# Rows of the delta rule's 16x16 blocks spread over their partitions by TensorE products in place of a round trip through DRAM

## Chip, cores and metric

One core of a Trainium2 chip. The metric is the device time in microseconds of one execution. TensorE is called PE here, VectorE DVE, ScalarE ACT, GpSimd POOL; SP only issues DMAs.

## What is computed

A trunk of two layers on 512 tokens of width 1024. The change lies in the first layer's mixer, in the chunked gated delta rule of its four heads. Cut to what matters here:

```
kk    = einsum('bhncd,bhnsd->bhncs', k * beta, k) * decay
a_mat = where(strictly lower, kk, 0) + eye
rhs   = concatenate([v * beta, k * beta * exp(gc)])
sol   = triangular_solve(a_mat, rhs, lower, unit_diagonal)
u, w  = sol[..., :dv], sol[..., dv:]
```

The rest of the layer (differential attention, output projection, MLP) and the second layer are the same code in both kernels.

## The kernel before

Weights come from HBM as float32, and ACT and DVE split each into a high and a low part in the fast matmul format (`whl`); a product is three matmuls of 512 or 256 columns. The trunk runs nearly all of its time on PE.

The first layer's mixer is `even_mixer` (lines 322 to 789). It is a list of generators that a planner at its end (lines 754 to 788) runs one step at a time while the program is built. `fill` holds the projections (q, k and v of the delta-rule heads: `project_a`, `values_a`; of the attention heads: `project_b`, `diff_values`; the output gates: `project_z`). `chains` holds the steps of each head. A chain's step says with `yield n` that its next step is due n * 1.55 us (`LAT_A`) of planned PE time later; `PE.time` (lines 82 to 94) adds up the matmuls' planned durations, four cycles a column for float32. Whenever no chain is due the planner takes a step of the next projection. So a `yield` decides how much projection work stands between two steps of a head. The order in which an engine then runs its instructions is near to this order, not equal to it: the building of the program moves an instruction ahead where its inputs and a buffer are there.

Four delta-rule heads work in pairs, 0 with 1 and 2 with 3. In `gdn_head`, line 502 finishes `lc`: for each of the 128 rows of a head's four token tiles, the 16 values of its row in the diagonal 16x16 block (128 partitions x 2 heads x 4 tiles x 16 columns). The second head of a pair then starts `small_inverses` for both (line 505). This inverts the 16x16 unit triangles by back substitution, and for it every partition needs all 16 rows of its block, not only its own: the tile `lb`, 128 partitions x 16 rows x 128 values. Before, `lb` is made by one DMA that writes `lc` to a DRAM tile `lsc` and eight DMAs that read it back, each broadcast to 16 partitions, all nine issued from ACT's queue (lines 435 to 441), followed by `yield 10.0`. Then 30 POOL instructions (lines 445 to 448), each needing the one before, turn `xc` into the inverses, with `lb` and `xc` as inputs; then `yield 10.0`, and the pair counts as solved. Its heads spread `xc` into block-diagonal tiles `x` on POOL (line 535, four instructions a head), PE transposes them (line 542), and three levels of products (line 551 on) join the blocks.

Things that share an engine or a buffer with this: the attention heads' rotation, of which one multiplication is on POOL (`rot`, line 706) between ACT's copies (line 702) and DVE's addition (line 707); the masks `ub` on POOL (lines 558, 563); `rs_t` on POOL (line 257); the tag `st` with five buffers (`N_ST`); the PSUM tag `ax` with two banks (`aux()`), which nearly every step of a delta-rule head uses.

Of the kernel before, what the change touches and what calls it, by code (L numbers as in the profile page):

```python
# [10 lines left out]
F32 = mybir.dt.float32  # L11
F32R = mybir.dt.float32r
I32 = mybir.dt.int32
AF = mybir.ActivationFunctionType
ALU = mybir.AluOpType
# [3 lines left out]
P = 128  # L19
# [17 lines left out]
BASE = 16  # L37
# [60 lines left out]
def trunk(ctx: ExitStack, tc: tile.TileContext, I, cst, out):  # L98
    nc = tc.nc
    V, S, G, PE = nc.vector, nc.scalar, nc.gpsimd, Tensor(tc)  # L100
# [10 lines left out]
    def acc():  # L111
        return pmm.tile([P, T], F32, tag="mm", name="mm")

    def aux():
        return pax.tile([P, T], F32, tag="ax", name="ax", bufs=2)
# [20 lines left out]
    def small(w, name):  # L136
        return smp.tile([P, w], F32, tag=f"sm{w}", name=name)
# [184 lines left out]
    def even_mixer(act, first, wba):  # L322
        w_in = I["w_in_even"][0]
        with ExitStack() as es:
# [4 lines left out]
            def st_(name):  # L329
                return gp.tile([P, T], F32, tag="st", name=name, bufs=N_ST)  # L330
# [1 line left out]
            def dtmp(name):  # L332
                return gp.tile([P, T], F32, tag="d", name=name, bufs=3)

            dp = es.enter_context(tc.tile_pool(name="dp", bufs=1, space=bass.MemoryType.DRAM))

            gmask = gp.tile([P, (N_MASK - 4) * P], F32, name="gmask")
            nc.scalar.dma_start(gmask, cst[:, 3 * P:(N_MASK - 1) * P])
            gm = {n: gmask[:, j * P:(j + 1) * P] for j, n in enumerate(CONST_NAMES[3:-1])}
# [8 lines left out]
            st, eye = {}, ccol[:, C_EYE:C_EYE + BASE]  # L348
# [84 lines left out]
            def small_inverses(pair):  # L433

                lc, n = small_l[pair], 2 * NT
                lsc = dp.tile([P // BASE, BASE * n * BASE], F32, tag="lsc", name="lsc", bufs=1)
                nc.scalar.dma_start(lsc.rearrange("b (r n) -> b r n", r=BASE), lc.rearrange("p h i c -> p (h i c)"))
                lb = gp.tile([P, BASE, n, BASE], F32, tag="lb", name="lb", bufs=1)
                for a in range(P // BASE):
                    nc.scalar.dma_start(lb[a * BASE:(a + 1) * BASE].rearrange("p r i c -> p (r i c)"),  # L440
                                        lsc[a:a + 1, :].broadcast_to([BASE, BASE * n * BASE]))
                yield 10.0
                xc = small_w[pair].rearrange("p h i c -> p (h i) c")
                tmp = gp.tile([P, n, BASE], F32, tag="xt", name="xt", bufs=1)
                for c in range(BASE - 1, 0, -1):
                    G.tensor_tensor(out=tmp[:, :, 0:c], in0=lb[:, c, :, 0:c],
                                      in1=xc[:, :, c].broadcast_to([P, n, c]), op=ALU.mult)
                    G.tensor_tensor(out=xc[:, :, 0:c], in0=xc[:, :, 0:c], in1=tmp[:, :, 0:c], op=ALU.add)
                yield 10.0
                solved.append(pair)  # L450

            def gdn_head(h, qT, kT):
# [51 lines left out]
                if second:  # L504
                    spawn(small_inverses(pair), 0.5)
# [268 lines left out]
            while chains or fill:  # L774
                due = [c for c in chains if c[0] <= PE.time]
                free = [f for f in fill if f[0]()]
                if due:
                    c = min(due, key=lambda c: c[0])
# [615 lines left out]
    with tc.tile_pool(name="ip", bufs=1) as ip:  # L1394
# [18 lines left out]
        ps = acc()  # L1413
# [3 lines left out]
        for i in range(NT):  # L1417
# [3 lines left out]
            r, ok, ss = small(1, "rx"), small(1, "ok"), ssx[:, i:i + 1]  # L1421
# [6 lines left out]
            if i == 2:  # L1428
                ps = acc()
# [10 lines left out]
        for k in range(KT):  # L1440
# [5 lines left out]
            w = cols[:, R_MIX + k:R_MIX + k + 1]  # L1446
# [9 lines left out]
    for layer in range(2):  # L1456
        if layer == 0:
            heads = even_mixer(act, first, wba)
            w, pairs = I["w_out_even"][0], (0, 2, 3, 1)
            xp = pools["x"] = ctx.enter_context(tc.tile_pool(name="xp", bufs=1))  # L1460
            for i in range(NT):
                x_tok.append(xp.tile([P, D], F32, name=f"x_tok{i}"))
                nc.sync.dma_start(x_tok[i], I["x"][0, i * P:(i + 1) * P, :])
        else:
            heads = odd_mixer(xs, last_tile)
            w, pairs = I["w_out_odd"][0], range(4)
        with tc.tile_pool(name=f"np{layer}", bufs=1) as pool:
            norm = Norm(pool, I["norm_mlp"][layer:layer + 1, :], 2)
            act, last_tile = out_proj(w, heads, norm, pairs)
        xs, halves, pj, last_tiles = mlp(layer, act, last_tile)  # L1470
        with tc.tile_pool(name=f"qp{layer}", bufs=1) as pool:
            if layer == 0:
                norm = Norm(pool, I["norm_mix"][1:2, :], 2)
            else:
                norm = Norm(pool, I["norm_final"].unsqueeze(0), 3)
            last_tile = ple(layer, xs, halves, pj, last_tiles, pool, norm)
# [24 lines left out]
```

## Time and profile before

| | us |
|---|---|
| median of 3 runs (1419.45 to 1420.86) | 1419.63 |
| the profiled execution, its own time | 1421.96 |
| span of the profiled execution, first to last instruction | 1420.2 |
| PE busy in it | 1384.1 (97%) |
| DVE busy | 867.3 (61%) |
| ACT busy | 773.5 (54%) |
| POOL busy | 174.2 (12%) |

Times in rows are microseconds from the start of the span. Matmuls overlap, and their ends are modelled, so that durations of neighbours can add up to more than their stretch: idle time of PE is read from the bracket of a row, and the price of a matmul from the distance between two starts. A bracket at the end of a row is the idle time of the engine before it and what ended it. In a stretch, "x" is the count of instructions that begin in it, and PEclk the share of full speed that the clock granted (1.00 is 2.4 GHz, 0.50 is 1.2 GHz). "PEld" is PE's weight load, "ACTq" an issue of a DMA by ACT's queue.

### The profile page before, as it was taken

To read this page: it belongs to the slowest core of one execution; us is meant where nothing else is said; L and a number is where in the kernel's file an instruction comes from. 1 tells how busy PE (TensorE), PEld (TensorE's weight loads), DVE (VectorE), ACT (ScalarE), POOL (GpSimd) and SP (SyncE) were. 2 spreads that over 40 slices of the span, in tenths; PEclk is the share of its full clock that TensorE was granted. 3 is DMA by queue.
4 is the path that set the end of the run, shared out by engine and by line. 5 is a ranking of instruction groups with operands and counts; after the bars stand their busy time and mean duration, and the time that the engine had idled before them with its cause. 6 is when DMAs were issued, how large, how long until landed. Compare 5 with 4: busy or idle time off the path is not lost. (4 is left out here: it accounts for less than half of the span.)

```text
span 1420.2 us, 18495 instructions
## 1 busy us (share of the span) xinstructions
PE 1384.1 (97%) x6969; PEld 1152.2 (81%) x6969; DVE 867.3 (61%) x1535; ACT 773.5 (54%) x1304; POOL 174.2 (12%) x231
## 2 busy tenths in 40 slices
PE   8999987999999999999999999999999999999997
PEld 6887775777888888888878888888888888888887
DVE  6837786665465665657665746646646565655865
ACT  6746775663555564556534545535355555554643
POOL 1350056010110201101001000000011020101100
PEclk9999998999999999999999999999999999999999
DMA  6251213114954856566333443852295476756611
GB/s 179 79 106 46 60 31 77 45 55 168 250 135 136 176 154 160 140 159 129 93 72 60 60 89 60 79 97 90 89 270 135 132 153 174 159 143 146 132 60 60
DMA packets 134238, 164.61 MB, mean 116 GB/s; under 512 B 9650, under 2 KB 91396, under 8 KB 133892
## 3 DMA queue, kind: packets, MB, share of 16 engines
q1 hardware_dynamic: 113968, 123.82, 32.6%
q0 software_dynamic: 15360, 33.56, 13.8%
q10 hardware_dynamic: 4820, 6.05, 1.9%
q8 instruction: 55, 0.90, 0.3%
q14 instruction: 35, 0.29, 0.1%
HBM read 152.78 MB, written 2.23 MB: 109 GB/s over the span
## 5 line engine op out<-in xcount | busy, mean ns | idle before, releaser
L90 PE MATMUL mm<-act,whl 128*128 128x512 f32 (+1 forms) x2784 | 657.9, 389 | 2.6 <-DVE whl L149 1.9
L90 PEld LDWEIGHTS mm<-act,whl 128*128 128x128 f32 x2784 | 506.3, 190 | 103.0 <-DVE whl L149 3.2
L90 PE MATMUL ax<-swhl,sa 128*128 128x512 f32 x1344 | 314.0, 389 | 0.0
L90 PEld LDWEIGHTS ax<-swhl,sa 128*128 128x128 f32 x1344 | 252.1, 188 | 52.4
L149 DVE TENSOR_TENSOR whl<-raw,whl 128x1024 fp32r<-128x1024 f32 x139 | 170.6, 1228 | 167.5 <-ACT whl L146 164.7
L149 DVE TENSOR_TENSOR swhl<-sraw,swhl 128x1024 fp32r<-128x1024 f32 x112 | 136.9, 1222 | 124.4 <-ACT swhl L146 124.2
L146 ACT ACTIVATE whl<-raw 128x1024 fp32r<-128x1024 f32 (+1 forms) x140 | 147.9, 1057 | 54.5 <-PE mm L90 50.2
L146 ACT ACTIVATE swhl<-sraw 128x1024 fp32r<-128x1024 f32 x112 | 118.8, 1060 | 101.2 <-PE ax L90 86.7
L90 PE MATMUL mm<-whl,act 128*128 128x256 f32 (+2 forms) x720 | 108.0, 307 | 0.2 <-ACT act L146 0.2
L1261 ACT ACTIVATE r<-mm 128x512 f32<-128x512 f32 x64 | 38.2, 597 | 126.0 <-PE mm L90 125.9
L90 PEld LDWEIGHTS mm<-whl,act 128*128 128x128 f32 x720 | 97.0, 190 | 6.7 <-ACT act L146 0.7
L1165 POOL DMA_DIRECT2D sraw<-w_mlp_down x48 | 57.5, 1218 | 251.0 <-DVE swhl L149 115.6
L319 DVE TENSOR_TENSOR x_tok<-x_tok,ax 128x512 f32<-128x512 f32 x114 | 73.5, 681 | 10.8 <-PE ax L90 10.7
L90 PE MATMUL mm<-owhl,act 128*128 128x256 f32 (+1 forms) x336 | 57.9, 329 | 0.0
L90 PE MATMUL mm<-owhl,hl 128*128 128x512 f32 x228 | 54.8, 397 | 0.0
L90 PEld LDWEIGHTS mm<-owhl,act 128*128 128x128 f32 x336 | 49.6, 188 | 6.4
L312 POOL TENSOR_TENSOR rn<-tn,nhalf 128x1 f32<-128x1 f32 x12 | 6.6, 553 | 385.9 <-DVE tn L311 385.9
L1165 POOL DMA_DIRECT2D sraw<-sraw x16 | 14.6, 915 | 302.5 <-DVE swhl L149 276.2
L90 PEld LDWEIGHTS mm<-owhl,hl 128*128 128x128 f32 x228 | 42.4, 188 | 10.1
L1174 ACT ACTIVATE sraw<-sraw 128x1024 f32<-128x1024 f32 x32 | 33.8, 1058 | 27.0 <-DVE swhl L149 17.5
L146 ACT ACTIVATE act<-ax 128x512 fp32r<-128x512 f32 x40 | 22.4, 595 | 43.1 <-PE ax L94 42.9
L149 DVE TENSOR_TENSOR sa<-hl,sa 128x512 fp32r<-128x512 f32 x64 | 43.8, 685 | 0.0
(341 smaller groups left out, 1609.6 us busy)
## 6 DMA issues: line engine op xcount, KB each, us to landing
raw<-w_mlp_up SPq DMA_DIRECT2D x64, 512.0 KB, 4.3
sraw<-w_mlp_down SPq DMA_DIRECT2D x64, 512.0 KB, 3.9
sraw<-w_mlp_down POOLq DMA_DIRECT2D x48, 512.0 KB, 5.8
raw<-w_in_even SPq DMA_DIRECT2D x32, 256.0 KB, 3.5
sraw<-sraw POOLq DMA_DIRECT2D x16, 512.0 KB, 6.3
raw<-w_ple_gate SPq DMA_DIRECT2D x16, 512.0 KB, 4.9
raw<-w_in_odd SPq DMA_DIRECT2D x16, 512.0 KB, 5.2
raw<-w_in_odd SPq DMA_DIRECT2D x32, 256.0 KB, 6.6
```

What stands on the lines that cost most here:

```text
L90: return self.tc.nc.tensor.matmul(out, lhsT=lhsT, rhs=rhs, start=start, stop=stop, skip_group_check=onto)
L146: S.activation(out=hi, in_=src, func=AF.Copy)
L149: return (E or V).tensor_tensor(out=lo, in0=src, in1=hi.bitcast(F32), op=ALU.subtract)
L312: G.tensor_tensor(out=r, in0=t, in1=nhalf[:, 0:1], op=ALU.pow)
L319: V.tensor_tensor(out=x_tok[i][:, cs], in0=x_tok[i][:, cs], in1=ps, op=op)
L1165: G.dma_start(o, t, accum_op=ALU.add)
L1174: S.activation(out=t, in_=t, func=AF.Copy, scale=-1.0)
L1261: S.activation(out=r, in_=ps, func=AF.Relu)
```

## The change

`lsc` and its DRAM pool, the nine DMAs and the `yield 10.0` behind them go. In their place `small_inverses` runs four rounds, for the quarters of the 16 rows from the last to the first. In a round DVE multiplies `lc`, repeated four times, by four columns of the (minus) identity that repeats every 16 partitions, so that in each partition only the copy of its own row is left (`own`, in a buffer of the tag `st`); PE multiplies that by the (minus) mask of the diagonal 16x16 blocks, which sums over the 16 partitions of a block, in float32 at 512 columns, into a bank of `ax`; ACT copies the bank into a quarter of `lb`; then `yield 0.3`. The back substitution and all that follows are unchanged.

```diff
             def small_inverses(pair):
 
                 lc, n = small_l[pair], 2 * NT
-                lsc = dp.tile([P // BASE, BASE * n * BASE], F32, tag="lsc", name="lsc", bufs=1)
-                nc.scalar.dma_start(lsc.rearrange("b (r n) -> b r n", r=BASE), lc.rearrange("p h i c -> p (h i c)"))
                 lb = gp.tile([P, BASE, n, BASE], F32, tag="lb", name="lb", bufs=1)
-                for a in range(P // BASE):
-                    nc.scalar.dma_start(lb[a * BASE:(a + 1) * BASE].rearrange("p r i c -> p (r i c)"),
-                                        lsc[a:a + 1, :].broadcast_to([BASE, BASE * n * BASE]))
-                yield 10.0
+
+                flat, w = lc.rearrange("p h i c -> p (h i c)"), n * BASE
+                for q in (3, 2, 1, 0):
+                    own = st_("own").rearrange("p (r c) -> p r c", r=4)
+                    V.tensor_tensor(out=own, in0=flat.unsqueeze(1).broadcast_to([P, 4, w]),
+                                    in1=eye[:, 4 * q:4 * q + 4].broadcast_to([P, 4, w]), op=ALU.mult)
+                    ps = aux()
+                    PE.matmul(ps, lhsT=gm["minus_base"], rhs=own.rearrange("p r c -> p (r c)"), start=True, stop=True)
+                    S.activation(out=lb[:, 4 * q:4 * q + 4].rearrange("p r i c -> p (r i c)"), in_=ps, func=AF.Copy)
+                    yield 0.3
```

## Rows read from the trace of the kernel before

**Rows 1.** The page: busy time, share of the span and instructions of each engine

```profile
PE 1384.1 (97%) x6969; PEld 1152.2 (81%) x6969; DVE 867.3 (61%) x1535; ACT 773.5 (54%) x1304; POOL 174.2 (12%) x231
```

**Rows 2.** PE's waits from 60 to 330 us: in total, times, longest

```profile
PE ax L94 <- POOL x L535: 7.1, 2, 6.8
PE ax L94 <- DVE u L649: 3.3, 3, 2.1
PE ax L90 <- DVE hl L720: 2.8, 1, 2.8
...
PE mm L90 <- DVE whl L149: 1.1, 1, 1.1
```

**Rows 3.** Stretches: length, busy time (instructions) of each engine, PEclk, DMA share, GB/s

```profile
109.20:115.40 6.20, 6.17 (x14) 4.29 (x14) 2.86 (x7) 3.27 (x6) 1.29 (x1) 0.50 0.33 89
...
213.20:234.70 21.50, 21.50 (x96) 16.15 (x96) 15.17 (x31) 14.83 (x31) 11.23 (x21) 1.00 0.56 125
234.70:241.40 6.70, 0.00 (x0) 0.00 (x0) 3.24 (x11) 1.82 (x4) 5.71 (x16) 0.78 0.00 1
241.40:255.40 14.00, 13.56 (x44) 10.36 (x45) 5.98 (x16) 7.64 (x15) 5.47 (x10) 0.50 0.01 2
255.40:300.00 44.60, 44.60 (x293) 35.06 (x292) 33.44 (x105) 30.23 (x76) 1.02 (x1) 1.00 0.15 48
```

**Rows 4.** Timeline, all engines, around the second pair's round trip: start, length, instruction

```profile
213.11 0.34 ACTq L437 DMA_DIRECT2D lsc<-lc  x1
214.69 0.31 ACTq L440 DMA_DIRECT2D lb<-lsc  x1
215.97 4.97 ACTq L440 DMA_DIRECT2D lb<-lsc  x5
220.98 1.19 ACT L702 ACTIVATE rot<-mm 32x512 f32<-32x512 f32 x2 [4.69 <-DMA raw<-w_in_even]
225.73 0.54 POOL L446 TENSOR_TENSOR xt<-lb,xc 128x120 f32<-128x120 f32 x1 [2.18 <-DMA lb<-lsc]
...
240.95 3.83 POOL L535 TENSOR_TENSOR x<-xc,gmask 128x128 f32<-128x128 f32 x8
241.45 0.48 PE L94 MATMUL ax<-gen,x 128*128 128x128 f32 x1 [6.75 <-POOL x L535]
242.31 0.94 PE L94 MATMUL ax<-gen,x 128*128 128x128 f32 x2 [0.38 <-POOL x L535]
```

**Rows 5.** Timeline around the first pair's round trip and what came behind it

```profile
70.20 0.34 ACTq L437 DMA_DIRECT2D lsc<-lc  x1
70.58 2.53 POOL L558 TENSOR_TENSOR ub<-u,gmask 128x512 f32<-128x512 f32 x2
81.83 0.40 POOL L446 TENSOR_TENSOR xt<-lb,xc 128x120 f32<-128x120 f32 x1 [7.90 <-DMA lb<-lsc]
92.78 2.40 ACT L702 ACTIVATE rot<-mm 32x512 f32<-32x512 f32 x4 [4.13 <-PE mm L90]
95.70 3.41 POOL L535 TENSOR_TENSOR x<-xc,gmask 128x128 f32<-128x128 f32 x8
99.05 1.31 POOL L706 TENSOR_TENSOR rot<-rot,sinr 128x512 f32<-128x512 f32 x1
100.39 0.69 DVE L707 TENSOR_TENSOR a<-a,rot 128x512 f32<-128x512 f32 x1 [4.49 <-POOL rot L706]
102.27 4.15 PE L90 MATMUL mm<-act,whl 128*128 128x512 f32 x17 [1.14 <-DVE whl L149]
109.23 0.55 PE L90 MATMUL ax<-hl 128*128 128x256 f32 x1 [2.81 <-DVE hl L720]
115.91 0.66 PE L94 MATMUL ax<-gen,x 128*128 128x128 f32 x4
```

**Rows 6.** Prices for the new instructions: PE's timeline, then the copies of one tile

```profile
62.71 1.05 PE L90 MATMUL ax<-kT 128*128 128x128 f32 x8
63.52 2.52 PE L90 MATMUL mm<-whl,act 128*128 128x256 f32 x19
...
L470 ACT ACTIVATE kd<-ax x4: 612/616/618, 51.8 to 205.6; 128x512 f32<-128x512 f32 x4
```

**Rows 7.** POOL's and DVE's timelines where both work at once

```profile
86.59 0.34 POOL L446 TENSOR_TENSOR xt<-lb,xc 128x80 f32<-128x80 f32 x1
88.72 1.40 POOL L448 TENSOR_TENSOR xc<-xc,xt 128x72 f32<-128x72 f32 x1
...
88.69 1.23 DVE L149 TENSOR_TENSOR whl<-raw,whl 128x1024 fp32r<-128x1024 f32 x1 [0.24 <-ACT whl L146]
```

More of the change, by code (lines that the diff above doesn't have):

```diff
@@ L333, in dtmp @@
                 return gp.tile([P, T], F32, tag="d", name=name, bufs=3)
-            dp = es.enter_context(tc.tile_pool(name="dp", bufs=1, space=bass.MemoryType.DRAM))
             gmask = gp.tile([P, (N_MASK - 4) * P], F32, name="gmask")
```

## The prediction

> **What bounds the kernel now.** I began with the page: PE is busy for 1384.1 of 1420.2 us [rows 1]. A wait is therefore worth something only where PE stands still for it, and each microsecond of new PE work costs about one. Next I read PE's waits in the mixer: its longest, 6.75 us, is for `x`, the tile that POOL makes from the inverses, and 2.8 and 1.1 us are for DVE (`hl`, `whl`) [rows 2]. The stretches then show what an idle PE costs besides: after the 6.75 us PE ran the 14.0 us from 241.4 to 255.4 at PEclk 0.50, and after the 2.8 us the 6.2 us to 115.4 [rows 3]. At half the clock a stretch full of matmuls loses half its length, so these two lost 7.0 and 3.1 us. From 255.4 on PE has no idle time again for 44.6 us, at the full clock [rows 3]: what is won before that is not won from a chain that ends last, it goes straight to the end.
>
> Now the round trip itself, in the timelines. For the second pair (heads 2 and 3) `lc` goes out at 213.11, and POOL's first instruction on `lb` starts at 225.73, with DMA as its releaser: 12.6 us [rows 4]. The first pair takes 70.20 to 81.83, 11.6 us [rows 5]. POOL's back substitution and `x` follow, and PE's transpose of `x` starts 28.3 us after `lc`, at 241.45, after the 6.75 us of waiting. Up to 234.7 PE had 21.5 us of other work in its queue [rows 3]. So for the second pair the chain lc, DRAM, `lb`, POOL, `x` is 6.8 us longer than what PE has to cover it.
>
> The first pair is different: its last `x` is made at 99.1 and PE takes it at 115.91, 16.8 us later [rows 5], so the trip is hidden. It costs something only through POOL: the rotation of the first attention head has its input from ACT at 95.2 but stands in POOL's queue behind substitution and `x` until 99.05, 3.9 us; DVE waits for it, DVE's split of the next weights is late, and PE stands for 1.14 us and then, for the same attention head's `hl`, 2.81 us [rows 5].
>
> So the whole loss in reach is 6.75 + 0.38 + 7.0 = 14.1 us for the second pair and 1.14 + 2.81 + 3.1 = 7.1 us for the first: 21.2 us.
>
> **The change part by part.** *New PE work.* Eight matmuls of 512 columns in float32. The rows have eight float32 passes of 128 columns, 1024 column passes, whose successor starts 0.81 us after them and which last 1.05 us with their tail [rows 6]. A float32 product of 512 columns is two passes, also 1024. So one costs 0.81 to 1.05; I take 0.87, nearer to the distance between starts since PE's neighbours overlap. Eight: 7.0 us (6.5 to 8.4), all on the path, as PE is full there.
>
> *New path to `lb`.* A round is a DVE multiplication of two SBUF operands at 128x512, 0.69 us by [rows 5] (`a`), the matmul, and an ACT copy from PSUM of 0.62 us [rows 6]. If DVE streams its four and the rest follows, 4 x 0.69 + 1.05 + 0.62 = 4.4 us; if banks or buffers let only one round go at a time, 4 x 2.36 = 9.4 us. I take 6, since two `ax` banks allow two rounds in flight but the other steps of two heads want them too. Against 12.6 and 11.6 us that is 6.6 and 5.6 us sooner. The Trainium skill ("DMA: Bandwidth & Descriptors", section "Anatomy of one DMA — SWDGE (gpsimd) path", the path of DMAs that POOL issues) gives about 2.0 us a DMA and bytes over 436 GB/s: for a write of 64 KB and, behind it, reads of 1 MB that is an estimate of 6.5 us; by it only 0.5 us would be won on the way to `lb`, and the sum would come out as a loss like the first rival's. The rows say 12.6 and 11.6, and the measurement decides.
>
> *DVE, ACT and POOL.* DVE gets 8 x 0.69 = 5.5 us and ACT 8 x 0.62 = 5.0 us; both are idle for some 30% of 213.2 to 234.7 [rows 3], so I cost the engines' own time at nothing. ACT loses 18 DMA issues; five of the second pair's stand in its queue for 4.97 us, and ACT's rotation copy starts when they are through [rows 4], so for that pair ACT is free some 4.7 us earlier. If the cover fails, a round's copy late by one weight split costs PE about 1 us. POOL's masks `ub` fill its queue for 2.5 us while it waits for DRAM in the first pair [rows 5]; since `lb` would come at about 76 they are still done by then (73.1). Where DVE and POOL work at once, a substitution step took 1.40 us against 0.34 for one step larger, with a DVE instruction on two SBUF operands from 88.69 beside it [rows 7]. The Trainium skill ("SBUF — State Buffer", section "Who interferes with whom") says that these two share a port pair as an exclusive lock; the trace agrees, 1.40 against 0.34. `own` is such an instruction: between 0 and 1.1 us a pair, inside the 6 us that I took.
>
> *The planner.* This is the part that the trace of before can't show. `yield 10.0` was 15.5 us of planned PE time; now there are 4 x 0.3 x 1.55 = 1.9 us and four matmuls planned at 0.85, together 5.3. So each pair's substitution, and all behind it, is planned 10.2 us earlier, with as much less projection work ahead of it. PE's queue between `lc` and `x` of the second pair would hold 21.5 + 3.5 = 25.0 us if the order stays, and 14.8 us if the whole shift comes through; the chain needs 28.3 - 6.6 = 21.7 us. So PE's wait there lies between 0 and 6.9 us. Half the shift leaves 19.9 us and a wait of 1.8 us, which I take: the rows can't favour an end. Waits of 1.14 us left the clock alone and one of 2.81 didn't [rows 3, 5], so I add half of that one's clock loss, 1.5. Second pair: 14.1 - 3.3 = 10.8 us won (0 to 14.1).
>
> For the first pair, `lb` at 76 and the same 17.3 us of POOL put the last `x` at 93.5, before the rotation's input at 95.2 (some 3.5 us later still, behind the new matmuls). So the 3.9 us in POOL's queue go, and with them the two PE waits. But the two heads' first level now lands in the same stretch as this rotation, on the same DVE and ACT; between 0 and 7.1 us of new waits. I take 2.6, about the size of the wait that goes. Won: 4.5 us.
>
> *Banks.* Eight more users of two `ax` banks: PE waits for an ACT copy between 0 and 0.62 us each, 0 to 5.0 in all; I take 1.
>
> *Sum*, against the profiled execution's own 1421.96: -10.8 - 4.5 + 7.0 + 1.0 = -7.3, so 1414.7. That execution is 2.3 us above the median of the runs shown, which gives 1412.3.
>
> **The rivals.** *The wait moves along (slower).* The order takes `x` up by the full 10.2 us, and PE stands for POOL in the second pair as it does now, 6.9 against 6.75 us, with the same fall of the clock. For it: PE's wait now ends on POOL's `x`, not on the DMA [rows 4], and after `lb` POOL still needs 15.7 us to the first `x`. Against: the new path takes no DRAM time that the order could misjudge. It decides from the point where PE's queue between `lc` and `x` falls below some 16 us. Price: +7.0 + 1.0 and, at best, -4.5 for the first pair: +3.5 to +8, 1423 to 1428.
>
> *Paid back (no change).* The second pair keeps half of its loss and the first wins nothing: -7 + 8 = +1, 1418 to 1422. For it: the round trip is hidden for the first pair by 16.8 us. The Trainium skill ("DMA: Bandwidth & Descriptors", section "Rules for kernel authors") has a rule against this change: issue a DMA early, wait late, and its fixed cost lies beside compute. By the trace that holds for the first pair only, and the second shows 6.75 us.
>
> *All of it.* PE finds `x` ready both times and the clock stays up: -21.2 + 7.0 to 8.0 = -13 to -14, 1406; other waits going with it, 1403.
>
> *It does not do what it says.* `own` takes buffers of `st`, five in all, that `ub` holds early; if each round waits for one, `lb` comes no sooner than from DRAM, and 1427 follows.
>
> **How the numbers follow.** Forecast 0.50 (own range 1407 to 1416), all of it 0.10, paid back 0.16, the wait moves along 0.20, not what it says 0.04. About 0.2%, 2.8 us, is what a measurement of this kernel can tell from no change. Faster is then 0.60, within it 0.16, slower 0.24. The range leaves out 0.1 or so at the slow end (half of the last two cases) and less at the fast one: 1404 to 1424. Predicted: 1412.
>
> **What would show it.** Right: POOL's first `xt` of a pair follows `lc` by 5 to 8 us; PE's wait for POOL `x` under 3 us; PEclk 1.00 for most of the 15 us behind it; `rot` of the first attention head starts when ACT's copies end; eight matmuls `ax<-own` at 0.8 to 1.05 us. Wrong: the wait for `x` at 6 us again (the order moved up), matmuls on `own` behind long waits for DVE or ACT (banks, `st`), or PE waits of a new kind among the levels of heads 0 and 1.

## The result: slower by 1%, outside the range

The changed kernel takes 1433.67 us (median of 4 runs, 1432.78 to 1434.71), the kernel before beside it 1419.93 (4 runs): ratio 1.0096, 95% interval 1.0079 to 1.0114. The forecast was 1412, with a range up to 1424. Its profiled execution took 1434.71 us with a span of 1432.9. The page, against [rows 1]:

```profile
PE 1394.2 (97%) x6985; PEld 1157.5 (81%) x6985; DVE 870.7 (61%) x1543; ACT 776.5 (54%) x1312; POOL 176.9 (12%) x231
```

PE is busy 10.1 us longer. The sixteen new passes (eight products) are these; in the form "duration min/median/max, first and last start":

```profile
L90 PE MATMUL ax<-own,gmask x16: 590/593/1223, 72.0 to 221.8; 128*128 128x512 f32 x16
L439 DVE TENSOR_TENSOR own<-lc,ccol x8: 677/680/1780, 70.9 to 214.4; 128x512 f32<-128x512 f32 x8
L443 ACT ACTIVATE lb<-ax x8: 597/597/599, 73.2 to 222.9; 128x512 f32<-128x512 f32 x8
```

PE's waits from 60 to 370 us, against [rows 2] (the code behind L441 moved down by two lines, so L537 is the L535 of before):

```profile
PE ax L94 <- POOL x L537: 6.6, 1, 6.6
PE ax L90 <- DVE vT L530: 3.5, 2, 2.8
PE ax L94 <- DVE do L944: 3.3, 2, 3.0
PE ax L94 <- DVE spare L315: 2.7, 1, 2.7
```

The wait for `x` is as long as it was (6.55 after 6.75 us, [rows 4]). The first pair's two waits, 1.14 and 2.81 [rows 5], are gone, but three of 2.7 to 3.0 us have come, for `vT` (with `own` behind it), `do` and `spare`; for the last two PE waited 1.0 and 0.8 us before. The stretches (columns as in [rows 3]):

```profile
98.00:115.00 17.00, 16.92 (x119) 13.98 (x119) 9.17 (x17) 13.03 (x24) 3.45 (x4) 1.00 0.13 33
...
226.90:233.40 6.50, 0.00 (x0) 0.00 (x0) 1.03 (x2) 0.00 (x0) 5.17 (x19) 0.79 0.22 73
233.40:251.00 17.60, 17.59 (x59) 13.95 (x60) 6.67 (x25) 5.79 (x14) 7.01 (x13) 0.50 0.00 1
251.00:300.00 49.00, 49.00 (x302) 38.61 (x301) 35.44 (x107) 34.63 (x83) 1.28 (x1) 1.00 0.13 44
...
323.60:330.00 6.40, 6.37 (x18) 5.20 (x19) 4.25 (x4) 3.53 (x4) 0.00 (x0) 0.52 0.59 194
```

98 to 115 us now runs at the full clock, as forecast. But after the wait for `x` PE runs 17.6 us at half speed where it ran 14.0 before [rows 3], and there is a second such stretch at 323.6, behind the new wait for `do`. The second pair's chain in the timelines of DVE, POOL and PE, in order of time:

```profile
208.54 0.23 DVE L504 TENSOR_TENSOR lc<-ax,lc 128x64 f32<-128x64 f32 x1
212.12 2.98 DVE L439 TENSOR_TENSOR own<-lc,ccol 128x512 f32<-128x512 f32 x3
214.50 1.74 POOL L708 TENSOR_TENSOR rot<-rot,sinr 128x512 f32<-128x512 f32 x1 [1.15 <-ACT rot L704]
216.19 0.40 POOL L448 TENSOR_TENSOR xt<-lb,xc 128x120 f32<-128x120 f32 x1
220.79 2.08 PE L90 MATMUL ax<-own,gmask 128*128 128x512 f32 x2 [2.76 <-DVE vT L530]
223.38 3.48 PE L90 MATMUL mm<-act,whl 128*128 128x512 f32 x13
232.91 3.32 POOL L537 TENSOR_TENSOR x<-xc,gmask 128x128 f32<-128x128 f32 x8
233.41 1.71 PE L94 MATMUL ax<-gen,x 128*128 128x128 f32 x4 [6.55 <-POOL x L537]
```

`xt` follows the end of `lc` by 7.4 us in place of 12.6, and `x` is 8.0 us sooner than before (232.91 after 240.95, [rows 4]). PE's own queue had moved up with it: the 13 matmuls at 223.38 are its last work ahead of `x`.

Where does such a kernel's stage end? Two chains close it: attention's last head, whose `do` VectorE scales, and the delta rule's last head (`u`). The last of each in DVE's timeline, for the kernel before and then for the changed one, with what PE did behind it:

```profile
299.48 0.69 DVE L937 SCALAR_TENSOR_TENSOR dsq<-dsq 128x512 f32<-128x512 f32 x1
...
308.08 0.68 DVE L939 TENSOR_REDUCE dss<-dsq 128x4 f32<-128x512 f32 x1
309.29 0.69 DVE L649 TENSOR_TENSOR u<-u,ro 128x512 f32<-128x512 f32 x1 [0.53 <-POOL ro L648]
312.25 0.69 DVE L942 TENSOR_TENSOR do<-do,dr 128x512 f32<-128x512 f32 x1
```

```profile
309.86 0.69 DVE L651 TENSOR_TENSOR u<-u,ro 128x512 f32<-128x512 f32 x1 [0.53 <-POOL ro L650]
...
319.45 0.69 DVE L939 SCALAR_TENSOR_TENSOR dsq<-dsq 128x512 f32<-128x512 f32 x1
320.18 0.69 DVE L941 TENSOR_REDUCE dss<-dsq 128x4 f32<-128x512 f32 x1
322.79 0.69 DVE L944 TENSOR_TENSOR do<-do,dr 128x512 f32<-128x512 f32 x1
...
323.63 1.09 PE L94 MATMUL ax<-gen,do 128*128 128x128 f32 x4 [2.99 <-DVE do L944]
352.77 1.22 PE L94 MATMUL ax<-gen,spare 128*128 128x128 f32 x8 [2.71 <-DVE spare L315]
```

Before, both chains ended within 3 us of each other, but attention was ready earlier: its `dsq` was done at 300.17, and the sum `dss` that follows it came at 308.08, behind the delta rule's last steps in DVE's queue. So there the delta rule set the end, and the last `do` came 2.97 us behind the last `u`. With the 3.3 us from `dsq` to `do` in the changed kernel, attention alone would have had its `do` at about 302.8 (an estimate). In the changed kernel the delta rule ends where it did, although its `x` came 8 us sooner, and attention, whose `dsq` now comes at 319.45, ends 10.5 us later. Its last head got its inputs late: the rotation's copies on ACT, four for each of its two tensors, begin at 243.66 and 259.73 after 223.29 and 229.50 before. Before, both came ahead of PE's wait for `x`; now both come behind it. The copies before, then after:

```profile
223.29 1.20 ACT L702 ACTIVATE rot<-mm 32x512 f32<-32x512 f32 x2
...
229.50 0.59 ACT L702 ACTIVATE rot<-mm 32x512 f32<-32x512 f32 x1
```

```profile
243.66 1.19 ACT L704 ACTIVATE rot<-mm 32x512 f32<-32x512 f32 x2
245.35 1.19 ACT L704 ACTIVATE rot<-mm 32x512 f32<-32x512 f32 x2
259.73 1.19 ACT L704 ACTIVATE rot<-mm 32x512 f32<-32x512 f32 x2 [0.20 <-PE mm L90]
```

From 60 us to PE's first transpose of `spare` (340.2 before, 352.8 after) the difference of 12.6 us splits into idle time of PE 18.9 to 22.3 (+3.4), time lost to the half clock 11.7 to 13.5 (+1.8), and work at the full clock 249.6 to 257.0 (+7.4, for the most part the rounds).

### The profile page after: what moved, and what is told of

Its sections match the earlier page's. It is cut to its first block, busy times and chain, and to the rows that moved or that the text cites. A ratio compares the mean times of both kernels' runs of the same rounds, so it can differ in the third digit from the quotient of the medians.

```text
span 1432.9 us, 18536 instructions
## 1 busy us (share of the span) xinstructions
PE 1394.2 (97%) x6985; PEld 1157.5 (81%) x6985; DVE 870.7 (61%) x1543; ACT 776.5 (54%) x1312; POOL 176.9 (12%) x231
## 4 chain that ended last, share of the span: by engine, by line
PE 84%; issue 4%; ACT 4%; DVE 4%; POOL 2%; DMA 1%; POOLq 0%; ACTq 0%; DVEq 0%
PE mm L90 52%; PE ax L90 28%; PE ax L94 3%; DMA raw<-w_ple_gate 1%; POOL xt L448 1%; DVE owhl L149 1%; ACT whl L146 0%; POOL xc L450 0%; DMA raw<-w_mlp_up 0%; ACT L408 0%; DVE whl L149 0%; POOL b L420 0%; ACT owhl L146 0%; POOL rs_t L257 0%; DVE spare L315 0%
## 5 line engine op out<-in xcount | busy, mean ns | idle before, releaser
L319 DVE TENSOR_TENSOR x_tok<-x_tok,ax 128x512 f32<-128x512 f32 x114 | 73.4, 679 | 10.8 <-PE ax L90 10.8
L146 ACT ACTIVATE act<-ax 128x512 fp32r<-128x512 f32 x40 | 22.4, 595 | 44.1 <-PE ax L94 44.1
```

The source lines that it names most:

```text
L146: S.activation(out=hi, in_=src, func=AF.Copy)
L319: V.tensor_tensor(out=x_tok[i][:, cs], in0=x_tok[i][:, cs], in1=ps, op=op)
```

## Experiments

One table serves all of them. "do" and "u" are the last start of each, read from DVE's timeline as above; the next column is the span less the later of the two. Ratios are against the kernel before on the same chip, whose median there was 1421.2 to 1421.8 in the rows from e1 on; kernels that ran on different chips are compared by these ratios.

| kernel | edit | median us | ratio, 95% | do | u | span less later |
|---|---|---|---|---|---|---|
| before | | 1419.9 | 1 | 312.3 | 309.3 | 1107.9 |
| after | the change | 1433.7 | 1.0096 (1.0079 to 1.0114) | 322.8 | 309.9 | 1110.1 |
| e1 | before, rounds beside DRAM, unused | 1420.3 | 0.9999 (0.9983 to 1.0016) | 308.8 | 305.8 | 1107.4 |
| e2 | before, plan short | 1426.7 | 1.0044 (1.0028 to 1.0060) | 313.7 | 303.8 | 1109.7 |
| e3 | after, plan put back | 1427.3 | 1.0042 (1.0027 to 1.0057) | 317.7 | 314.8 | 1107.6 |
| e4 | after, substitution cut | 1421.8 | 1.0002 (0.9993 to 1.0011) | 311.2 | 298.2 | 1109.4 |
| e5 | e3, rot on DVE | 1413.6 | 0.9945 (0.9930 to 0.9960) | 303.7 | 300.7 | 1109.6 |
| e6 | after, rot on DVE | 1433.2 | 1.0083 (1.0063 to 1.0102) | 324.2 | 311.2 | 1110.1 |
| e7 | rounds for the first pair only | 1428.0 | 1.0050 (1.0033 to 1.0067) | 314.9 | 311.9 | 1109.0 |
| e8 | after, substitution on DVE | 1431.4 | 1.0074 (1.0054 to 1.0095) | 320.0 | 307.1 | 1107.5 |
| e9 | before, rot on DVE | 1414.6 | 0.9955 (0.9944 to 0.9967) | 302.8 | 299.9 | 1108.8 |
| e10 | e5, rounds trimmed | 1413.9 | 0.9943 (0.9927 to 0.9960) | 301.9 | 298.9 | 1109.7 |
| e11 | after, plan back, first pair | 1430.8 | 1.0063 (1.0042 to 1.0084) | 323.2 | 311.2 | 1106.2 |
| e12 | after, plan back, second pair | 1422.4 | 1.0006 (0.9996 to 1.0015) | 313.0 | 310.0 | 1106.6 |
| e13 | after, longer plan behind it | 1427.2 | 1.0038 (1.0023 to 1.0053) | 317.1 | 314.1 | 1107.8 |
| e14 | e13, rot on DVE | 1413.3 | 0.9938 (0.9921 to 0.9954) | 305.2 | 302.2 | 1107.9 |
| e15 | e12, rot on DVE | 1433.2 | 1.0077 (1.0062 to 1.0092) | 318.7 | 315.7 | 1109.8 |
| e16 | before, longer plan | 1426.3 | 1.0041 (1.0026 to 1.0055) | 295.4 | 314.1 | 1110.4 |
| e17 | before, substitution cut | 1409.8 | 0.9915 (0.9900 to 0.9930) | 300.0 | 297.0 | 1107.8 |
| e18 | e5, substitution cut | 1415.1 | 0.9955 (0.9939 to 0.9972) | 304.8 | 301.8 | 1106.9 |

The last column lies between 1106.2 and 1110.4 in all twenty rows, while the spans differ by 26.5 us: to within 4.2 us the span follows the later of these two instructions. In 13 of the twenty rows the last `do` starts 2.96 to 2.97 us behind the last `u`, as in the kernel before. In six (the changed kernel, e2, e4, e6, e8, e11) it comes 10 to 13 us behind it, and attention ends the stage; in e16 `do` comes well ahead.

**Work or order?** Theory A at this point: the loss is the rounds' PE work and an order of the queues that counts on `x` too early. Theory B: the rounds' own waits. e1 is the kernel before with the four rounds added (into a buffer that nobody reads) and the plan as it was:

```
+ (the four rounds, their copy into own)
+ yield 6.6
```

> The kernel before with the change's four rounds beside it: lb still comes from DRAM, the rounds' result goes back into their own buffer and is not used, and the planned time up to the substitution is kept at 15.5 us (four rounds planned at 5.3, then yield 6.6). Theory A (the rounds cost their PE work, the rest of the loss comes from the planned time that fell by 10.2 us a pair): +7 to +9 us against the kernel before, 1427 to 1429. Theory B (the rounds cost all of it, by waits for DVE, ACT, banks and buffers of st besides the work): +12 to +14 us, 1432 to 1434.

1420.3 us, no change: both theories missed. The eight products cost nothing on balance: the order that came out had no wait for `x` at all. POOL's timeline shows a second difference that mattered later, a rotation that slipped in between the substitution's instructions:

```profile
223.06 0.36 POOL L455 TENSOR_TENSOR xt<-lb,xc 128x96 f32<-128x96 f32 x1
223.38 1.28 POOL L715 TENSOR_TENSOR rot<-rot,sinr 128x512 f32<-128x512 f32 x1
224.62 0.38 POOL L457 TENSOR_TENSOR xc<-xc,xt 128x96 f32<-128x96 f32 x1
```

e2 is the reverse, the plan's shift without the rounds:

```
- yield 10.0
+ yield 3.4
```

> The kernel before, lb from DRAM, with yield 3.4 (5.3 us planned) in place of yield 10.0 (15.5 us): the change's shift of the plan alone, no rounds. Theory A: PE reaches x earlier while x comes no sooner, a wait for POOL x of over 7 us, and attention head 3 ends later: +4 to +9 us, 1424 to 1429. Theory B: within 2 us of the kernel before.

+5.5 us, by A. PE waits for POOL's `x` for 13.05 us at 230.8. A second wait, 4.08 us at 103.2, also stands ahead of a transpose of `x`, but by the view for ACT's copy `z`; `x` was made by 99.2. Moving the order up without moving the work costs, with no product added.

e3 puts the planned time back into the changed kernel:

```
      yield 0.3
+ yield 6.6
```

> The changed kernel with a further yield 6.6 behind its four rounds, so that the substitution is planned as late as before (15.5 us). Theory A: the 7.4 us of PE work stay, the wait for POOL x of the second pair falls under 3 us, attention head 3 is no longer last: 1418 to 1426. Theory B: as the changed kernel, 1431 to 1435.

1427.3, just past A's range: 0.54 of the lost 0.96% come back, and the wait for `x` is gone. But 11.54 us of another kind stand in its place. POOL, DVE and PE in order of time:

```profile
228.36 3.32 POOL L538 TENSOR_TENSOR x<-xc,gmask 128x128 f32<-128x128 f32 x8
231.64 1.26 POOL L709 TENSOR_TENSOR rot<-rot,sinr 128x512 f32<-128x512 f32 x1
232.94 0.69 DVE L710 TENSOR_TENSOR a<-a,rot 128x512 f32<-128x512 f32 x1 [11.08 <-POOL rot L709]
235.94 0.55 PE L90 MATMUL ax<-hl 128*128 128x256 f32 x1 [11.54 <-DVE hl L723]
```

`x` is early, and useless: a rotation of attention waits behind the whole substitution in POOL's queue, DVE stands for it for 11.08 us, and PE for DVE.

e4 leaves 2 of the 30 substitution instructions in the changed kernel:

```
- for c in range(BASE - 1, 0, -1):
+ for c in range(BASE - 1, BASE - 2, -1):
```

> The changed kernel with 2 of the 30 POOL instructions of a pair's substitution (the other 14 columns are left out, so the inverses are not computed): x is there some 12 us sooner. Theory A: PE's wait for x and the low clock behind it go, 10 to 15 us less than the changed kernel, 1419 to 1424; attention head 3 stays last. If the wait for x is not what costs the time (theory B), 1430 to 1434.

1421.8, by A: 0.94% less than the changed kernel, 13.4 us, is what POOL's substitution costs there, with PE's order re-dealt from the second pair's `x` on. Alone this reads as the whole loss; e17 below corrects that.

**What stands behind the substitution.** From e3's trace the theory became: POOL's 15 to 17 us are one block, and the cost is whatever waits for it or behind it. Its rival D: any new order costs some 5 to 10 us through attention's last head. e5 and e6 move the rotation's product:

```
- G.tensor_tensor(out=rot, in0=rot, in1=sinr, op=ALU.mult)
+ V.tensor_tensor(out=rot, in0=rot, in1=sinr, op=ALU.mult)
```

> This is e3 (the changed kernel with the planned time put back) with the rope's product rot*sinr (L709) on VectorE in place of GpSimd. In e3 x was ready at 231.6 us, 9 us sooner than before, and TensorE waited 11.54 us all the same, because rot stood behind x in GpSimd's queue (rot at 231.64, VectorE's add at 232.94, hl at 235.4). Theory A (what costs is which work the 15 us substitution on GpSimd has behind it or waiting for it): the wait of 11.5 us and its half-speed stretch go, 1412 to 1420 us. Rival D (any new order of the queues costs some 5 to 10 us, through attention head 3, whatever the wait is): 1424 to 1431 us, no change against e3.

> The changed kernel itself with rot*sinr on VectorE. Here TensorE waited for x itself (6.55 us at 233.4), and rot stands behind x on GpSimd but nothing has to wait for it longer than for x. Theory A: the wait for x stays at 4 to 8 us and the time at 1428 to 1436 us. If GpSimd's queue as a whole were the cost (rot before and behind the substitution), 1418 to 1425 us. Rival D: 1428 to 1440 us.

e5: 1413.6, 13.7 us under e3 and 0.55% under the kernel before. The second pair's stretches, e3's first and then e5's:

```profile
215.00:230.00 15.00, 9.02 (x40) 6.35 (x39) 4.14 (x7) 4.62 (x7) 13.11 (x34) 0.91 0.12 35
230.00:245.00 15.00, 9.06 (x21) 5.93 (x22) 6.61 (x17) 5.85 (x12) 4.17 (x7) 0.52 0.12 35
```

```profile
215.00:230.00 15.00, 14.19 (x61) 10.06 (x59) 11.48 (x23) 10.35 (x18) 13.35 (x27) 1.00 0.24 70
230.00:245.00 15.00, 14.41 (x73) 11.05 (x72) 14.23 (x32) 11.41 (x23) 6.27 (x13) 1.00 0.12 37
```

POOL is busy about as long in both (17.3 and 19.6 us); PE's busy time goes from 18.1 to 28.6 of 30 us and its clock stays up. e6, with the plan still short, gains nothing (1433.2): PE waits for `x` itself for 6.05 us, and for a `do` 5.96 us. So with the rounds in place, a gain over the kernel before took both edits.

**Which pair?** e7 has the rounds for the first pair alone; e11 and e12 put the planned time back for one pair:

```
+ if pair == 0:        (e12: pair == 1)
+     yield 6.6
```

> The rounds for the first pair of heads only; the second pair goes through DRAM with the planned 10.0 us, as before. Theory A (the loss lies in the second pair, where TensorE waits for x): the first pair keeps what it gains (1.14 + 2.81 us of waits and the half-speed stretch of 109 to 115 us, less 3.5 us of TensorE work), 1414 to 1421 us. If the loss is shared by both pairs: 1424 to 1430 us.

> The changed kernel with the planned 6.6 us put back for the first pair alone. Of the 6 to 7 us that e3 gained by putting it back for both, Theory A2 (both pairs' substitutions are planned too early; the first pair's x, moved ahead of four attention blocks, pushes attention back, and the second pair costs its wait for x): 1424 to 1430 us. If only the second pair matters: 1432 to 1436 us.

> The changed kernel with the planned 6.6 us put back for the second pair alone. Theory A2: the direct wait for x goes but attention head 3 stays late, since the first pair's x keeps its early place: 1424 to 1431 us. If only the second pair matters: 1424 to 1428 us as in e3, with TensorE's wait of 10 us for rot behind the substitution. If only the first matters: 1432 to 1436 us.

e7 lost 6.8 us where A had a gain (its time lies in the other theory's range): the first pair's waits went, but with DRAM for the second pair PE waits 5.62 us for its `x`, and the delta rule and attention both end 2.6 us late. On the changed kernel e11 gains 0.33%, and e12 0.90%, which is more than both at once (e3, 0.54%). Neither time lies in any range set for it: e11 is between its two, e12 under all three. The parts don't add up; each edit deals the queues anew. All that the two numbers say is that the second pair weighs more.

**The substitution on VectorE** (e8: `V` for `G` in L448 and L450):

> The changed kernel with the 30 instructions of the substitution (L448, L450) on VectorE in place of GpSimd. On GpSimd they took 15 to 17 us from xt to x, held up by VectorE's two-input instructions; on VectorE 30 instructions of 0.2 to 0.35 us, some 8 us. Theory A (the length of the substitution and what queues behind it on GpSimd): x of the second pair 5 to 8 us sooner, no wait for x, 1412 to 1422 us. Rival E (VectorE's queue, busy 0.92 of the time at 215 to 230 us in the changed kernel, passes the delay to rot, own and do): TensorE waits for VectorE 6 us or more in its place, 1428 to 1440 us.

1431.4: rival E by its time, though PE's longest wait is only 2.9 us. DVE and POOL in the second pair:

```profile
218.16 0.75 DVE L448 TENSOR_TENSOR xt<-lb,xc 128x120 f32<-128x120 f32 x1
...
240.35 0.17 DVE L450 TENSOR_TENSOR xc<-xc,xt 128x8 f32<-128x8 f32 x1
...
241.91 4.22 POOL L537 TENSOR_TENSOR x<-xc,gmask 128x128 f32<-128x128 f32 x8
```

One instruction takes 0.17 to 0.75 us, but each waits its turn among attention's: 22.4 us from first to last, longer than POOL's 16.7.

**Are the rounds worth anything?** e9 moves the rotation in the kernel before; e10 cuts e5's rounds to the columns that are read (512, 384, 256, 128 in place of 4 x 512).

> The kernel before (round trip through DRAM, plan of 10.0 us) with rot*sinr on VectorE. It tells whether the 7.6 us by which e5 beats the kernel before come from the rounds at all. Theory A (e5 gains since the rounds make x early and, with rot off GpSimd, nothing stands behind it): here lb still lands 12 us after lc, TensorE still waits 4 to 8 us for x, 1416 to 1423 us. Rival F (e5's gain is that of the moved rot alone): 1411 to 1416 us, within 2 us of e5.

> e5 (1413.6 us) with each round cut to the columns that the substitution reads: row r needs only columns under r, so the four rounds of a pair carry 512, 384, 256 and 128 columns in place of 4 x 512 (the rest of lb stays unwritten and unread). Theory A (the rounds' only price is their TensorE time, 8 x 0.9 us for both pairs at 512 columns): 37% of 7 us less, 1410 to 1412.5 us, if the order of the queues holds. Rival D (another order of the queues outweighs it): 1414 to 1420 us. If that work is hidden: 1413 to 1414.5 us.

e9 takes 1414.6, 0.1% from e5: rival F holds, and the gain over the kernel before is the moved rotation's, not the rounds'. e9 still waits for `x`:

```profile
234.26 1.71 PE L94 MATMUL ax<-gen,x 128*128 128x128 f32 x4 [7.87 <-POOL x L535]
```

e5 has that wait no more, and eight products more. e10's products fell to 275 to 697 ns a pass as meant, yet its time is e5's (1413.9), as the case "hidden" had it. Its order is a new one, with a wait of 6.45 us for `hl` at 223.7, so e10 doesn't tell hidden work from work that another wait replaced.

**Plan or place in the queue?** e13 lengthens the second yield, behind the substitution, from 10.0 to 16.6; e14 is e13 with the rotation on DVE, e15 is e12 with it, and e16 gives the kernel before 12.0 and 16.6. (These are the plan's units, 1.55 us of PE time each; 16.6 is 25.7 us, so "what the trace showed" in the texts below is too long, and e16 tests a longer plan rather than a true one.)

> The changed kernel; only the second yield, behind the 30 instructions of the substitution, is 16.6 in place of 10.0 (in its trace they took 16.7 us from the first xt to x). So GpSimd gets the substitution as early as in the changed kernel, and x is planned 6.6 us later, as in e3. Theory P (the loss is that TensorE's order counts on x earlier than it can be there): the wait of 6.55 us for x and its half-speed stretch go, head 3 of attention is sooner, 1417 to 1424 us. Rival Q (rot then stands behind the substitution in GpSimd's queue, as in e3): a wait of 8 us or more for rot in its place, 1425 to 1432 us.

> e13 with rot*sinr on VectorE. Theory P with Q out of the way: no wait for x and none for rot, 1409 to 1415 us, as e5 (1413.6). If TensorE's order costs by itself: 1418 to 1432 us.

> e12 (1422.4 us: the planned 6.6 us put back for the second pair only) with rot*sinr on VectorE. In e12 x is there at 237.2 and rot behind it, TensorE waits 5.24 us at 243.1 for p of attention. Theory P: that wait goes, 1411 to 1417 us. Rival R (the early first pair costs 5 us or more by its place ahead of attention, whatever rot does): 1418 to 1424 us.

> The kernel before, with the plan told what the trace showed: 12.0 us for the round trip in place of 10.0, 16.6 us for the substitution in place of 10.0; rot stays on GpSimd. Theory P: the wait of 6.75 us for x and the half-speed stretch behind it go, 1410 to 1418 us. Rival Q (something else then waits behind the substitution): 1418 to 1427 us.

e13 went by Q, with 10.67 us of waiting for `hl`, and e14 by P. e13 has the same order on PE as e3, e14 as e5, and their ratios agree within 0.07% (1.0038 and 1.0042, 0.9938 and 0.9945). So here the order sets the time, not the yield by which it came about, and the same order gives the same time. e15 was slower than either theory had it, 1433.2. Its trace shows other waits than those the theories were about: a POOL instruction, `rs_t` of 1 us, stands inside the substitution, and the scaling of `do` behind it on DVE; then PE waits for `x` itself. Which of the two costs how much was not isolated. POOL, DVE, then PE twice:

```profile
224.48 1.02 POOL L257 TENSOR_TENSOR rs_t<-rs_t,nhalf 128x4 f32<-128x4 f32 x1
225.53 0.25 DVE L258 TENSOR_TENSOR dr<-rs_t,rs_ok 128x4 f32<-128x4 f32 x1 [5.11 <-POOL rs_t L257]
227.15 1.11 PE L94 MATMUL ax<-gen,do 128*128 128x128 f32 x4 [5.98 <-DVE do L946]
234.32 1.71 PE L94 MATMUL ax<-gen,x 128*128 128x128 f32 x4 [6.06 <-POOL x L539]
```

e16 (Q) shows the other side: attention ends at 295.4, 17 us sooner than before, but the delta rule at 314.1, and the kernel is 4.5 us slower by the median.

**How much was in reach?** e17 and e18 cut the substitution, as e4 did, in the kernel before and in e5.

> The kernel before with 2 of the 30 instructions of the substitution (its inverses are not computed); the round trip through DRAM and the plan stay. It tells what the kernel before could gain at most from an earlier x, which the forecast put at 21.2 us in reach (14.1 for the second pair, 7.1 for the first). If the forecast's sizing of that gain was right: 1400 to 1409 us. If the end of the stage is set by attention's head 3 (its do at 312 us beside the last u of the delta rule at 309), an earlier x gains less: 1411 to 1420 us.

> e5 (1413.6 us: rounds, planned time put back, rot on VectorE) with 2 of the 30 instructions of the substitution (its inverses are not computed). If GpSimd's substitution is out of the way there, as its trace shows (no wait for x, none for rot above 1 us): 1411 to 1415 us, no change. If it still costs: 1404 to 1410 us.

e17 gains 11.8 us (0.85%), just past the end of the range for 21.2 us in reach, with 2.86 us of waiting for `x` left at 222.4 (DRAM and POOL's `x` are still there); e18 gains nothing. So POOL's substitution costs 0.85% before, 0.94% after, equal within their intervals, and nothing in e5. The last is the cleanest of the three: e18 has e5's order on PE, ACT and DVE up to 400 us, while e17's, like e4's, was re-dealt from the second pair's `x` on. And since it costs about the same before and after, the substitution is not what makes the two kernels differ.

## Why the prediction was wrong

- **What bounds the kernel: right in kind, incomplete.** PE's waits and the half clock behind them were the loss. But "goes straight to the end" took the order as given: in the kernel before the delta rule does set the end, but attention, by the estimate above, leaves room for some 9 us only. The change moved attention's last head back instead. In the changed kernel `x` was 8.0 us sooner and the last `u` 0.6 us later; the last `do`, which the prediction never looked at, was 10.5 us later. I had read the stretch from 255.4 to 300, where PE is never idle, and concluded that order no longer mattered there.
- **The planner: the step that failed.** I took half of the shift, a wait of 1.8 us. The chain from the end of `lc` to PE's `x` took 24.6 us (208.8 to 233.4) where I had 21.7: 7.4 us to the first `xt` in place of 6, with a rotation of 1.74 us ahead of it in POOL's queue, and 17.2 us from there to PE's `x` where the kernel before had 15.7. PE's work and small waits between took 18.1 us (208.8 to 226.9) where I had 19.9. These 2.9 and 1.8 us are the whole step from 1.8 to 6.55 us. The second pair, forecast at 10.8 us won, won nothing: its wait and its half-speed stretch are as long as before or longer. e4 and e17 give POOL's substitution the same price in both kernels, some 12 to 13 us; and of the 21.2 us in reach e17 found 11.8 with a wait of 2.86 still there.
- **The rival "the wait moves along": right mechanism, too cheap.** It forecast 6.9 us of waiting and got 6.55, with the same fall of the clock, at 1423 to 1428; and it came with 18.1 us in PE's queue, not under the 16 that I had set for it. Measured: 1433.7. Missing is attention's last head behind it, with the `do` wait, the half speed at 323.6 and the wait for `spare`. With the substitution cut in both kernels 0.88% still separate them (1.0002 and 0.9915), 12.5 us, nearly the whole loss. If PE's new work costs there the 7.4 us of the account above, some 5 remain for these new waits; that share is a remainder, not measured by itself.
- **New path to `lb`: right for the first quarter, by luck for the rest.** 7.4 us for the second pair and 4.3 for the first (`lc` written by 69.57, `xt` at 73.82) against 6 forecast with 4.4 to 9.4 as bounds, and 12.6 and 11.6 by DRAM. But this is the time to the first quarter of `lb`, which is all that the first `xt` reads. The four rounds took 14.7 us for the second pair (ACT's last copy ends at 223.51) and 8.9 for the first: for the second pair that is longer than the trip through DRAM. POOL did not wait for it, since the substitution takes the quarters one by one. The 2.98 us that DVE took for three `own` in the chain above, against 0.68 for one alone, is 0.9 us more than three alone, within the 0 to 1.1 us that I had priced for the lock.
- **New PE work: right, 7.0 forecast, 7.4 counted.** Four passes in a row (75.80 us) took 1.98 us with the tail of the last, so a product is at most 0.99 us, within 0.81 to 1.05. Of the 1.0 us that I had added for banks, the trace shows one wait of 0.67 us for a copy `lb`. What these products cost in the end depends on what they displace: nothing in e1, nothing in e5 against e9, some 0.4% (5.7 us, rotation on DVE in the one, on POOL in the other) between e18 and e17. The order differs in each of these pairs too, so none prices the products alone.
- **First pair: right in its steps, wrong in its worth.** Both waits and the half-speed stretch went, and from 60 to 170 us PE has no wait over 0.8 us. Yet e7, with this alone, is 6.8 us slower. The first pair's delta rule ended 15 us sooner (last `u` at 174.4 after 189.6), and the second pair's 2.6 us later. Which of the re-dealt queues costs the 6.8 us was not isolated.
- **"Paid back":** the Trainium skill ("DMA: Bandwidth & Descriptors", section "Rules for kernel authors") would issue a DMA early and wait late. With the rotation off POOL the two paths are level, e9 (DRAM) 1414.6 and e5 (rounds) 1413.6. So the times agree with the rule, but the trace does not show the trip hidden: e9 still waits 7.87 us at `x`.
- **"It does not do what it says":** no, as far as the time goes. The first quarter of `lb` came sooner, and no wait for a buffer of `st` is among PE's waits.

The cause, as far as it is shown: the order that followed from the shorter plan. The rounds with the old plan, their result unused, cost nothing (e1, 0.9999), the shorter plan without the rounds costs 0.44% (e2), both together 0.96%, and with the planned time put back for the second pair the rounds are level with the kernel before (e12, 1.0006). The 0.5% by which both together exceed the sum of the two is not taken apart. POOL's substitution, the block that something stands behind in e3 and e15, has about the same price in both kernels; it is not the difference between them, which stays at 0.88% with it cut. Also not shown: why a given plan yields the order it does. e14, the fastest with the rounds (0.9938), and e9, the fastest without (0.9955), differ by less than their intervals.

## What to carry to other kernels

Before a producer is made faster, look for the instructions on other engines that are queued behind its longest block, and for the second chain that ends beside the one you shorten: here moving one line's product, 1.3 us a time, off POOL gained 0.45%, some 7 us, in the kernel before, and the change itself lost 13.7. Where a planner orders the queues by estimated times, a faster step is also a new order: run the new step with the old plan, and the old step with the new plan, before judging either.

## What the runs showed of the hardware

The length of the half-speed stretch did not follow the length of the wait ahead of it. After 6.55 us of waiting the changed kernel ran 17.6 us at 0.50; after 11.54 us e3 ran at 0.50 from 235.9 to 243 and at the full clock from 246; after 7.87 us e9 ran at 0.50 to 242 and at 0.91 until 246. PE was busy throughout all three. What set the length is open. e3's stretches:

```profile
235.90:240.00 4.10, 4.06 (x9) 2.52 (x9) 2.06 (x5) 2.40 (x5) 0.00 (x0) 0.50 0.41 126
240.00:243.00 3.00, 3.00 (x9) 2.12 (x8) 1.27 (x6) 1.28 (x5) 1.27 (x1) 0.50 0.00 0
243.00:246.00 3.00, 3.00 (x11) 2.11 (x10) 1.36 (x5) 0.69 (x1) 0.00 (x0) 0.78 0.00 0
```

The DVE multiplication `own`, on two SBUF operands, took up to 1.78 us beside a POOL multiplication, 0.68 alone. The first of the three `own` at 212.12 is the one of 1.78 us, and it began beside this:

```profile
212.08 1.27 POOL L560 TENSOR_TENSOR ub<-u,gmask 128x512 f32<-128x512 f32 x1 [4.36 <-ACT sqq L520]
```

The Trainium skill ("SBUF — State Buffer", section "Who interferes with whom") has the two share a port pair as an exclusive lock; the trace agrees, on DVE's side as it did on POOL's in [rows 7].
